# One-core streaming encoder layer: the second block's summed activations formed in the output projection, first column blocks taken out of their banks unscaled, the merge add on VectorE

## The chip, the cores and the metric

The kernel runs on one core of one Trainium2 chip. The metric is the device time of one execution in microseconds. A profile is one separate execution; its rows are times from the start of its span. TensorE (PE) does the matmuls, VectorE (DVE), ScalarE (ACT) and GpSimd (POOL) the elementwise work, SyncE (SP) starts the transfers (DMA). Each engine works through its own list of instructions strictly in order.

## The reference

560 rows (16 meta tokens, 512 prompt rows, 32 sample rows) of 1024 features pass through one layer, all in float32. Cut to what matters here:

```python
def half_step_ffn(x, g, w_gate, w_up, w_down):          # D_MODEL 1024, D_FF 2816
    h = rms_norm(x, g)
    return x + 0.5 * ((silu(h @ w_gate) * (h @ w_up)) @ w_down)
...
x = half_step_ffn(x, ffn1_norm, ffn1_w_gate, ffn1_w_up, ffn1_w_down)      # block 1
... # h @ w_in_all, short convolution, multi-head latent attention
conv_branch = (b_gate * conv_y) @ w_conv_out
mla_branch = attn @ w_mla_out
merged = sigmoid(g_conv) * conv_branch + sigmoid(g_mla) * mla_branch
x = x + merged @ w_out_all                                                # output projection
x = half_step_ffn(x, ffn2_norm, ffn2_w_gate, ffn2_w_up, ffn2_w_down)      # block 2
```

## The kernel before, in words

The residual lies transposed: `y[p, k, t]` holds feature 128k+p of row t, k = 0..7. Block 1 works on all 560 columns in two halves of 280, the output projection and block 2 on 544 columns in two halves of 272.

**Three matmuls for one.** Each float32 operand is split into a rounded part and a rest (`split`, L113: ACT casts the high part, `V.tensor_sub` or GpSimd subtracts for the low part), and `mm3` (L159 to L162) multiplies wh·xh, wh·xl and wl·xh. A weight tile is loaded and split by `load` (L117): DMA `wr`, ACT `wh`, DVE `wl` (128x1024).

**The RMS norm is applied late.** `gained` (L499) leaves gain·y as xh, xl and adds up squares (POOL, `sq`); the factor of each row, 1/rms, comes out of `token_rstd` (L512) and a Newton iteration into `r` (L172 to L178). `spread` (L180) turns `r` into a tile `R` that has the factor on all partitions: matmuls against the identity (L184), then copies out of two banks (L188 to L193). A product of unscaled activations is multiplied by R when it leaves its bank.

**A feed-forward block** is `ffn` (L198). Its 22 blocks of 128 hidden columns make 11 pairs. Pair 0 goes through `plain` (L229): column block j = 0 (gate and up side by side, two accumulators, 96 matmuls), then j = 1 (again 96). In it `before(0)` and `before(1)` are calls of the stage around: in block 1 `before(1)` transposes `craw` and `qkr` (L628, L631), in block 2 it is `spread`; block 1's own spread is at L606, ahead of `before`. Behind each j the banks are emptied by

```python
V.tensor_mul(two(tg), ps[0][:, :, :n], Rv)       # L255: waits for R
S.activation(tg, tg, AF.Silu)
V.tensor_mul(two(tu), ps[1][:, :, :n], two(tg))  # L257
split(ah[:, j], al[:, j], tu)
```

Pairs 1 to 10 go through `job` (L345): one gate job and one up job a pair, seven Winograd products of 12 matmuls instead of eight. Its moving operands are sums of activations, made once a block by `combine` (L264): ACT forms gain·y for k and k+4 into a `tg` tile, DVE makes four sums (L272 to L275), and `split` writes them to xsh, xsl (128x1120 or 128x1088); four combines a block. Its weight sums `ws`, `yl`, `zl` are DVE and ACT work of `operands` (L301). `up_job` (L386) multiplies and splits the result into ah, al, with the subtraction on GpSimd, in three pieces for 544 or 560 columns. `down` (L401) multiplies chunks of pairs with w_down; the last chunk closes each block of y (L430, L431). Behind block 1's last chunk, `done` (L633) also loads `wkv` into the place of xsh and scales it in eight DVE instructions (L651).

**Merge** (L1204). A loop over m = 0..7 makes attn @ w_mla_out (48 matmuls), then

```python
V.tensor_mul(two(sg), ps, two(sg))   # L1243: gate times the branch
GP.tensor_add(sg, sg, cb)            # L1244: plus the convolution branch
split(mh[:, m], ml[:, m], sg)
```

GpSimd also multiplies both gates by R2 and the convolution branch by its gate. The output projection (L1247 to L1252) then takes m = 0..7, k = 0..7 each, and adds `yo`, the residual.

**What sets the order.** The order on each engine is fixed when the program is built, by a scheduler; where the code says "later" it is bound by hand.

Of the kernel before, what the change touches and what calls it, by code (L numbers as in the profile page):

```python
# [1 line left out]

# [10 lines left out]
F32 = mybir.dt.float32  # L13
# [8 lines left out]
P = 128  # L22
# [28 lines left out]
WMAX = KD * P  # L51

# [25 lines left out]
def encoder_step(ctx: ExitStack, tc: tile.TileContext, i, o):  # L78
# [101 lines left out]
    def spread(pa, pb, rstd, R, n=MS, meta_first=False):  # L180
# [12 lines left out]
        V.tensor_copy(R[:, MS:], pa)  # L193
# [4 lines left out]
    def ffn(pool, acc, one, wg, wu, wd, gain, lo, y, R, w0, before, done):  # L198
# [11 lines left out]
        xs = (xh, xl)  # L210
        a = {}
# [7 lines left out]

        def gates():  # L220
            return pool.tile([P, 2, N2], F32, tag="tg", name="tg", bufs=2)
# [7 lines left out]
        def plain(p):  # L229

            ah, al = pair_tiles(p)
            for j in range(2):
                fc = slice(j * P, (j + 1) * P)
                if j == 0:
                    w = w0 or [load([x[:, fc]]) for x in (wg, wu)]
                    ps = [acc(), acc()]
                    order = [(k, q) for k in range(KD) for q in range(2)]
                    if w0:
                        order = [(k, q) for q in range(2) for k in range(KD)]
                    for s, (k, q) in enumerate(order):  # L240
                        for e in range(2):
                            mm3(ps[e][:, q, :n], at_k(w[e], k), at_k(xs, k, cols[q]), k == 0, k == KD - 1)
                        if s == 7:
                            before(0)
                    before(1)
                else:
                    ps = []
                    for x in (wg, wu):
                        w = load([x[:, fc]])
                        ps.append(acc())  # L250
                        for k in range(KD):
                            for q in range(2):
                                mm3(ps[-1][:, q, :n], at_k(w, k), at_k(xs, k, cols[q]), k == 0, k == KD - 1)
                tg, tu = rows(), rows()
                V.tensor_mul(two(tg), ps[0][:, :, :n], Rv)  # L255
                S.activation(tg, tg, AF.Silu)
                V.tensor_mul(two(tu), ps[1][:, :, :n], two(tg))  # L257
                split(ah[:, j], al[:, j], tu)
                yield

        xsh = pool.tile([P, KH, 4, n], F32R, tag="xsh", name="xsh")
        xsl = pool.tile([P, KH, 4, n], F32R, tag="xsl", name="xsl")

        def combine(k):  # L264

            z = gates()
            for j in range(2):
                m = k + j * KH
                S.activation(z[:, j], y[:, m, lo:], AF.Identity, scale=cT[:, gain + m : gain + m + 1])
            c = gates().rearrange("p a (b n) -> p (a b) n", n=n)  # L270
            b11, b12, b21, b22 = (z[:, j // 2, (j % 2) * n : (j % 2 + 1) * n] for j in range(4))
            V.tensor_sub(c[:, 0], b11, b12)  # L272
            V.tensor_sub(c[:, 2], b22, b12)
            V.scalar_tensor_tensor(c[:, 1], c[:, 0], -1.0, b22, op0=ALU.mult, op1=ALU.subtract)
            V.scalar_tensor_tensor(c[:, 3], c[:, 1], -1.0, b21, op0=ALU.mult, op1=ALU.subtract)  # L275
            return split(xsh[:, k], xsl[:, k], c)[1]
# [24 lines left out]
        def operands(raw, after=None):  # L301
# [17 lines left out]
            if after:  # L319
                for x in steps:  # L320
                    tc.add_manual_dep(x.ins, after.ins.name, NOSYNC, reason="later")
# [49 lines left out]

        G = {}

        def gate_job(p, ops):
            def into():
                G[p] = gates()
                return lambda j: G[p][:, j]

            def finish():
                g = G[p]  # L380
                V.tensor_mul(g, g, R[:, None, lo:].to_broadcast([P, 2, N2]))
                S.activation(g, g, AF.Silu)

            return job(p, ops, finish, into)

        def up_job(p, ops):  # L386
# [71 lines left out]
        first = plain(0)  # L458
        next(first)
        for k in range(KH):  # L460
            last = combine(k)
        next(first)
        raws = [fetch(*jobs[0][1:])]
        ops = operands(raws[0], last)
# [3 lines left out]
        for x, (make, w, p) in enumerate(jobs):  # L468
            g = make(p, ops)
# [5 lines left out]
            d = None  # L475
            if make is gate_job and ready:
                d = down(ready, False)
                next(d)
                ready = None
            if x + 1 < len(jobs):  # L480
                ops = operands(raws[x + 1])
# [56 lines left out]
    with ExitStack() as es:  # L538
# [15 lines left out]
        with tc.tile_pool(name="ps0", bufs=4, space=PSUM, reuse_waits="tile") as psum:  # L554
# [43 lines left out]
            for t, step in enumerate((3, 5, 8, 10, 6)):  # L598
                junk = pool.tile([P, D], F32, tag="tg", name="junk", bufs=2)
# [6 lines left out]
            spread(px(), px(), r1, R1, MS, True)  # L606
# [6 lines left out]
        def before(step):  # L613
# [11 lines left out]
            else:  # L625
                n = CC + 16
# [5 lines left out]
                V.tensor_copy(gqk[:QK], ps[:QK, :2])  # L632

        late = {}

        def done(m):
            if m == 0:
                late["yms"] = pool.tile([P, KD, MS], F32, tag="zh", name="yms")
                late["sq"] = pool.tile([P, T], F32, tag="xsl", name="sq")
                late["tmp"] = pool.tile([P, T], F32, tag="tg", name="sqt", bufs=2)  # L640
# [13 lines left out]
        ffn(pool, acc, one, wg, wu, wd, G1, 0, y, R1, w0, before, done)  # L654
# [690 lines left out]
```

## Time and profile before

| | |
|---|---|
| time before, median of 3 runs | 1450.91 us (1448.59 to 1451.77) |
| the profiled execution | 1446.04 us, its span 1444.1 us |
| TensorE | busy 1394.5 us, 97% of the span; granted clock 0.99 in the mean |
| VectorE | 1001.0 us, 69% |
| ScalarE | 652.3 us, 45% |
| GpSimd | 492.8 us, 34% |

Times inside the profile are counted from the start of its span. TensorE's matmuls overlap, so how fast they go is read from how many start in a stretch, not from the duration of one. A granted clock of 1.00 is 2.4 GHz, of 0.50 1.2 GHz.

### The profile page before, as it was taken

The page shows a single profiled execution, that of the slowest core. Times are in us where ns is not written, and L with a number is a line of the kernel's source. Part 1 is how long each engine was busy: PE and PEld are TensorE (multiplying, and loading weights), DVE is VectorE, ACT ScalarE, POOL GpSimd, SP SyncE. Part 2 cuts the span into 40 slices and gives each one's busy share as a digit, 9 for nine tenths or more (in the row PEclk, how much of TensorE's full clock was granted, in tenths as well). Part 3 has the DMA queues.
Part 4 walks back from the last instruction along what each step waited for, and adds up shares of the span by engine and source line. Part 5 has one row for each costly group of instructions (what it writes and reads, how often), then busy time and mean ns, then how long its engine had stood idle before and what let it go on. Part 6 is the DMA issues. An engine that isn't in the chain of part 4 may idle for free.

```text
span 1444.1 us, 26675 instructions
## 1 busy us (share of the span) xinstructions
PE 1394.5 (97%) x10667; PEld 1360.9 (94%) x10667; DVE 1001.0 (69%) x1703; ACT 652.3 (45%) x1220; POOL 492.8 (34%) x731
## 2 busy tenths in 40 slices
PE   7999999999999999999999999998989999999998
PEld 5899999999899999998999999998989999999988
DVE  5887878787566665955955857533587787878744
ACT  6543443434324454453554556533364343434431
POOL 1011111112396864645623424179811021111120
PEclk9999999999999999999999999999999999999999
DMA  6242323233243222222332234355433232324213
GB/s 172 65 125 74 115 66 113 75 102 88 78 131 93 84 79 77 71 60 56 119 90 71 84 120 145 113 175 159 143 95 103 72 107 87 118 68 125 69 44 95
DMA packets 215634, 141.63 MB, mean 98 GB/s; under 512 B 6415, under 2 KB 202914, under 8 KB 215510
## 3 DMA queue, kind: packets, MB, share of 16 engines
q1 hardware_dynamic: 215510, 139.93, 32.8%
q8 instruction: 83, 1.36, 0.4%
q14 instruction: 41, 0.34, 0.1%
HBM read 124.15 MB, written 15.76 MB: 97 GB/s over the span
## 4 chain that ended last, share of the span: by engine, by line
PE 79%; POOL 7%; DVE 6%; issue 4%; DMA 2%; ACT 1%; SPq 0%; POOLq 0%; ACTq 0%; DVEq 0%
PE b L160 9%; PE b L161 9%; PE b L162 9%; PE acc L160 7%; PE acc L161 7%; PE acc L162 7%; PE f L160 6%; PE f L161 6%; PE f L162 6%; POOL sg L71 2%; POOL sq L71 1%; PE t L160 1%; PE t L1168 1%; POOL cb L71 1%; PE late L160 1%
## 5 line engine op out<-in xcount | busy, mean ns | idle before, releaser
L71 POOL TENSOR_TENSOR al<-tu,ah 128x187 fp32r<-128x187 f32 (+3 forms) x120 | 106.5, 919 | 612.7 <-issue 374.5
L114 ACT CAST wh<-wr 128x1024 fp32r<-128x1024 f32 (+2 forms) x165 | 166.6, 1019 | 235.5 <-PE acc L161 128.0
L160 PE MATMUL f<-xh,wh 128*128 128x272 f32 (+1 forms) x816 | 240.2, 295 | 1.5 <-DVE ext L838 1.2
L162 PE MATMUL f<-xh,wl 128*128 128x272 f32 (+1 forms) x816 | 239.1, 293 | 0.0
L161 PE MATMUL f<-xl,wh 128*128 128x272 f32 (+1 forms) x816 | 238.6, 293 | 0.0
L161 PE MATMUL acc<-al,wh 128*128 128x280 f32 (+1 forms) x704 | 203.9, 291 | 2.6 <-POOL al L71 2.6
L160 PE MATMUL acc<-ah,wh 128*128 128x280 f32 (+1 forms) x704 | 203.1, 291 | 2.4 <-DVE tu L430 1.5
L162 PE MATMUL acc<-ah,wl 128*128 128x280 f32 (+1 forms) x704 | 202.9, 291 | 0.3 <-DVE wl L115 0.3
L71 POOL TENSOR_TENSOR wl<-wr,wh 128x256 fp32r<-128x256 f32 x196 | 151.9, 804 | 150.0 <-ACT wh L114 131.1
L115 DVE TENSOR_TENSOR wl<-wr,wh 128x1024 fp32r<-128x1024 f32 (+2 forms) x115 | 141.4, 1236 | 37.4 <-ACT wh L114 32.9
L160 PEld LDWEIGHTS f<-xh,wh 128*128 128x128 f32 x816 | 154.8, 190 | 2.8 <-ACT wh L114 1.4
L161 PEld LDWEIGHTS f<-xl,wh 128*128 128x128 f32 x816 | 154.9, 190 | 0.4
L162 PEld LDWEIGHTS f<-xh,wl 128*128 128x128 f32 x816 | 154.8, 190 | 0.5
L160 PE MATMUL b<-xsh,yh 128*128 128x280 f32 (+1 forms) x480 | 139.1, 290 | 0.7 <-ACT kept L342 0.5
L161 PE MATMUL b<-xsl,yh 128*128 128x280 f32 (+1 forms) x480 | 139.1, 290 | 0.0
L162 PE MATMUL b<-xsh,yl 128*128 128x280 f32 (+1 forms) x480 | 138.9, 289 | 0.1
L161 PEld LDWEIGHTS acc<-al,wh 128*128 128x128 f32 x704 | 132.4, 188 | 3.1 <-POOL al L71 3.0
L160 PEld LDWEIGHTS acc<-ah,wh 128*128 128x128 f32 x704 | 132.0, 188 | 3.4 <-DVE tu L430 1.9
L162 PEld LDWEIGHTS acc<-ah,wl 128*128 128x128 f32 x704 | 132.0, 188 | 0.6 <-DVE wl L115 0.6
L115 DVE TENSOR_TENSOR yl<-ws,yh 128x1024 fp32r<-128x1024 f32 x80 | 103.4, 1293 | 38.0 <-ACT yh L114 37.7
L114 ACT CAST yh<-ws 128x1024 fp32r<-128x1024 f32 x80 | 84.0, 1050 | 92.5 <-PE b L161 84.8
L161 PE MATMUL b<-xl,wh 128*128 128x280 f32 (+1 forms) x320 | 92.5, 289 | 0.0
(358 smaller groups left out, 3826.3 us busy)
## 6 DMA issues: line engine op xcount, KB each, us to landing
wr<-in_w_in_all_dram SPq DMA_DIRECT2D x43, 512.0 KB, 3.9
wr<-in_ffn_w_down_dram SPq DMA_DIRECT2D x32, 512.0 KB, 4.3
wr<-in_ffn_w_gate_dram SPq DMA_DIRECT2D x23, 512.0 KB, 3.9
wr<-in_ffn_w_up_dram SPq DMA_DIRECT2D x23, 512.0 KB, 5.1
wq<-in_ffn_w_gate_dram SPq DMA_DIRECT2D x20, 512.0 KB, 4.2
wq<-in_ffn_w_up_dram SPq DMA_DIRECT2D x20, 512.0 KB, 4.2
wr<-in_ffn_w_down_dram SPq DMA_DIRECT2D x16, 384.0 KB, 3.5
gt_dram<-b SPq DMA_DIRECT2D x16, 272.0 KB, 2.0
```

Of the source, the lines that this page charges most:

```text
L71: last = op(out[:, lo:hi], a[:, lo:hi], b[:, lo:hi])
L114: a = S.copy(hi, src)
L115: return a, (E or V).tensor_sub(lo, src, f(hi))
L160: PE.matmul(out, a[0], b[0], start=start, stop=False, skip_group_check=onto)
L161: PE.matmul(out, a[0], b[1], start=False, stop=False, skip_group_check=onto)
L162: PE.matmul(out, a[1], b[0], start=False, stop=stop, skip_group_check=onto)
L1168: PE.transpose(ps[:, (t - j) * P : (t - j + 1) * P], pw[:, a : a + P], ident)
```

## The change

1. `combine` is pulled out of `ffn` into `summed`. For block 2 the four combines are made in the output projection, which takes its blocks in the order 0, 4, 1, 5, 2, 6, 3, 7: after each second one, features k and k+4 are there. `tg` has three buffers instead of two.
2. The first two projections (m = 0 and 4) are both opened with k = 0..6; k = 7 follows for each.
3. `plain` copies the banks of column block 0 to SBUF unscaled (`S.copy` for gate, `V.tensor_copy` for up) and multiplies by R later; `before(1)`, with the spread of both blocks in it, stands inside column block 1 (behind k = 3 of gate). Block 1's combines come behind the copies of R.
4. Block 1's first gate job (pair 1) is `plain_job`: 96 plain matmuls instead of 84.
5. The merge add is a VectorE instruction. The last up job's `al` is subtracted on VectorE in both blocks.
6. `next(d)`, the load of down's first weights, stands ahead of the gate job.

```diff
+OUT_ORDER = (0, 4, 1, 5, 2, 6, 3, 7)
...
+    def summed(pool, gain, lo, y):
...
+        def combine(k, after=None):
+            z = gates()
...
+            for j in range(2):
+                m = k + j * KH
+                S.activation(z[:, j], y[:, m, lo:], AF.Identity, scale=cT[:, gain + m : gain + m + 1])
+            c = gates().rearrange("p a (b n) -> p (a b) n", n=n)
...
+            made.append(split(xsh[:, k], xsl[:, k], c)[1])
+            if after:
+                for x in made:
+                    tc.add_manual_dep(x.ins, after.ins.name, NOSYNC, reason="later")
...
+            g, u = rows(), rows()
+            S.copy(two(g), ps[0][:, :, :n])
+            V.tensor_copy(two(u), ps[1][:, :, :n])
...
+                    if x is wg and k == 3:
+                        ready = before(1)
+                if x is wg:
+                    V.tensor_mul(g, g, R[:, lo:])
+                    S.activation(g, g, AF.Silu)
+                    V.tensor_mul(u, u, g)
+                    split(ah[:, 0], al[:, 0], u)
+                    ready = [c(ready) for c in combine]
...
+        def plain_job(p, w, finish, into):
+
+            out = into()
+            for j in range(2):
+                ops = load([w[:, (2 * p + j) * P : (2 * p + j + 1) * P]])
+                ps = acc()
+                for k in range(KD):
+                    for q in range(2):
+                        mm3(ps[:, q, :n], at_k(ops, k), at_k(xs, k, cols[q]), k == 0, k == KD - 1)
+                S.copy(two(out(j)), ps[:, :, :n])
+                yield
...
-                    split(ah[:, j], al[:, j], u[j], GP)
+                    split(ah[:, j], al[:, j], u[j], V if p == NF // 2 - 1 else GP)
...
-            spread(px(), px(), r1, R1, MS, True)
...
+                last = spread(one("b1"), one("b2"), r1, R1, MS, True)
...
-            GP.tensor_add(sg, sg, cb)
+            V.tensor_add(sg, sg, cb)
...
-        for m in range(KD):
-            ps = project(i["w_out_all"][0, :, m * P : (m + 1) * P], (mh, ml))
...
+        for j, m in enumerate(OUT_ORDER):
+            if j == 0:
+                opened = [project(w_out(x), (mh, ml), 0, KD - 1) for x in (0, 4)]
+            if j < 2:
+                ps = project(None, (mh, ml), KD - 1, KD, opened[j])
+            else:
+                ps = project(w_out(m), (mh, ml))
...
+            if j % 2:
+                combine[j // 2]()
```

VectorE at the start of block 1, before: `tg`, `xsl` are a combine's tiles, `wl_495` a weight, `acc_278` the gate bank of column block 0, `b_385` and `b_388` the transposes of `before(1)`.

```order
L115 TENSOR_TENSOR wl_495<-wr_493,wh_494 128x1024
L193 COPY R1_84<-px_261 128x512
L115 TENSOR_TENSOR xsl_275<-tg_401,xsh_274 128x1120
L188 COPY R1_84<-px_262 128x48
L272 TENSOR_TENSOR tg_411<-tg_408 128x280
L273 TENSOR_TENSOR tg_411<-tg_408 128x280
L255 TENSOR_TENSOR tu_391<-acc_278,R1_84 128x560
L629 COPY cT_70<-b_385 128x59
L632 COPY gqk_78<-b_388 96x2
```

The same place in the changed kernel, from the last step of the Newton iteration (L180); `acc_270` is the up bank of column block 0.

```order
L180 SCALAR_TENSOR_TENSOR r1_75<-nrb_250,r1_75 128x5
L550 MEMSET ms_4680 128x5
L278 COPY tu_377<-acc_270 128x560
L664 COPY cT_70<-b_420 128x59
L667 COPY gqk_78<-b_423 96x2
L117 TENSOR_TENSOR wl_497<-wr_495,wh_496 128x1024
L195 COPY R1_84<-b1_411 128x512
L218 TENSOR_TENSOR tg_458<-tg_455 128x280
```

The bank is emptied ahead of the copies of R, the transposes' copies too, and no combine stands ahead of any of them.

VectorE at the end of block 1, before: `tu_4037`, `tu_4038` are the last up job's two results, `acc_4145` the first bank of the last `down` chunk.

```order
L396 TENSOR_TENSOR tu_4037<-tu_4037,tg_3905 128x560
L368 TENSOR_TENSOR tu_4038<-b2_4036,kept_4110 128x280
L396 TENSOR_TENSOR tu_4038<-tu_4038,tg_3905 128x560
L651 TENSOR_SCALAR wkv_4257<-wkv_4257,cT_70 128x160 x8
L430 SCALAR_TENSOR_TENSOR tu_4251<-acc_4145,R1_84 128x560
L430 SCALAR_TENSOR_TENSOR tu_4278<-acc_4214,R1_84 128x560
```

The same place in the changed kernel.

```order
L433 TENSOR_TENSOR tu_4028<-tu_4028,tg_3896 128x560
L391 TENSOR_TENSOR tu_4029<-b2_4027,kept_4101 128x280
L433 TENSOR_TENSOR tu_4029<-tu_4029,tg_3896 128x560
L117 TENSOR_TENSOR al_4188<-tu_4028,ah_4187 128x560
L687 TENSOR_SCALAR wkv_4244<-wkv_4244,cT_70 128x160 x8
L117 TENSOR_TENSOR al_4188<-tu_4029,ah_4187 128x560
L467 SCALAR_TENSOR_TENSOR tu_4238<-acc_4136,R1_84 128x560
```

Both subtractions for `al` are now on VectorE, one ahead of the eight instructions on `wkv`, one behind them.

VectorE in the changed kernel from the second to last output block (`late_12340` is its bank) on: combine 3 of block 2 (`tg_12469`) lies between the residual adds and the weights of block 2.

```order
L1303 TENSOR_TENSOR y_11285<-late_12340,yo_12389 128x544
L117 TENSOR_TENSOR wl_12494<-wr_12492,wh_12493 128x1024
L538 SCALAR_TENSOR_TENSOR xl_74<-y_11285,cT_70,xh_73 128x544
L218 TENSOR_TENSOR tg_12469<-tg_12466 128x272
L1303 TENSOR_TENSOR y_11285<-late_12406,yo_12455 128x544
L117 TENSOR_TENSOR wl_12624<-wr_12622,wh_12623 128x1024
L538 SCALAR_TENSOR_TENSOR xl_74<-y_11285,cT_70,xh_73 128x544
L219 TENSOR_TENSOR tg_12469<-tg_12466 128x272
```

And further on, where column block 0 of block 2 is emptied (`acc_12499` is its up bank, `r3` the row factors):

```order
L117 TENSOR_TENSOR yl_12772<-ws_12758,yh_12771 128x1024
L178 TENSOR_TENSOR nra_12594<-r3_77 128x5
L278 COPY tu_12619<-acc_12499 128x544
L179 SCALAR_TENSOR_TENSOR nrb_12595<-nra_12594,ms_12585 128x5
L117 TENSOR_TENSOR wl_12693<-wr_12691,wh_12692 128x1024
L180 SCALAR_TENSOR_TENSOR r3_77<-nrb_12595,r3_77 128x5
L117 TENSOR_TENSOR wl_12760<-wr_12753,wh_12759 128x1024
L178 TENSOR_TENSOR nra_12594<-r3_77 128x5
```

Before, the combines and the copies of R stood between this bank's last matmul and its emptying; now one weight's low part (`yl_12772`) stands ahead of the copy.

## Rows read from the trace of the kernel before

**Rows 1.** The page, part 1: span, and each engine's busy time, share and instructions.

```profile
span 1444.1 us, 26675 instructions
...
PE 1394.5 (97%) x10667; PEld 1360.9 (94%) x10667; DVE 1001.0 (69%) x1703; ACT 652.3 (45%) x1220; POOL 492.8 (34%) x731
```

**Rows 2.** Windows: us; busy of PE, PEld, DVE, ACT, POOL; granted clock; DMA; GB/s.

```profile
...
37.03:43.86 6.83, 5.79 (x26) 5.79 (x26) 6.11 (x13) 3.66 (x5) 0.00 (x0) 0.50 0.12 35
100.00:120.00 20.00, 20.00 (x157) 20.00 (x157) 14.47 (x18) 5.38 (x6) 0.00 (x0) 1.00 0.30 86
960.00:980.00 20.00, 20.00 (x162) 20.00 (x161) 8.35 (x8) 7.43 (x10) 20.00 (x30) 1.00 0.63 192
999.59:1006.42 6.83, 4.99 (x22) 4.99 (x23) 2.54 (x3) 1.95 (x3) 6.83 (x11) 0.50 0.55 161
1067.86:1071.27 3.41, 3.41 (x17) 3.41 (x16) 2.77 (x5) 2.60 (x3) 0.00 (x0) 0.50 0.00 0
```

**Rows 3.** Waits of TensorE, 30 to 40 us: total us, times, longest.

```profile
...
PE b L628 <- DVE R L188: 2.1, 1, 2.1
PE acc L160 <- DVE tu L255: 1.0, 1, 1.0
```

**Rows 4.** Timeline of TensorE, 31 to 39 us: start, us, instruction, [idle before].

```profile
...
33.10 1.48 PE L184 MATMUL px<-ident,r 128*128 128x128 f32 x10 [0.46 <-DVE ms L515]
...
38.08 0.60 PE L160 MATMUL acc<-xh,wh 128*128 128x280 f32 x1 [1.03 <-DVE tu L255]
```

**Rows 5.** Waits of TensorE, 380 to 388 us.

```profile
...
PE acc L161 <- POOL al L71: 1.3, 1, 1.3
PE acc L160 <- DVE tu L430: 0.8, 1, 0.8
```

**Rows 6.** Waits of TensorE, 990 to 1003 us.

```profile
...
PE late L160 <- ACT mh L114: 5.4, 1, 5.4
```

**Rows 7.** Waits of TensorE, 1048 to 1095 us.

```profile
...
PE acc L160 <- DVE tu L255: 2.7, 1, 2.7
...
PE b L184 <- DVE r L178: 1.0, 1, 1.0
```

**Rows 8.** Timeline of TensorE, 1399 to 1405 us.

```profile
...
1403.02 0.40 PE L161 MATMUL acc<-al,wh 128*128 128x272 f32 x1 [1.26 <-POOL al L71]
```

**Rows 9.** Timeline of VectorE, 30 to 40 us.

```profile
...
35.14 1.31 DVE L115 TENSOR_TENSOR xsl<-tg,xsh 128x1120 fp32r<-128x1120 f32 x1
```

**Rows 10.** Timeline of VectorE, 380 to 392 us.

```profile
...
383.59 2.82 DVE L651 TENSOR_SCALAR wkv<-wkv,cT 128x160 f32<-128x160 f32 x8 [1.49 <-DMA wkv<-in_w_in_all_dram]
386.33 1.38 DVE L430 SCALAR_TENSOR_TENSOR tu<-acc,R 128x560 f32<-128x560 f32 x2
```

**Rows 11.** Timeline of VectorE, 1060 to 1082 us.

```profile
...
1066.82 0.43 DVE L272 TENSOR_TENSOR tg<-tg 128x272 f32<-128x272 f32 x1
...
1069.31 0.73 DVE L115 TENSOR_TENSOR al<-tu,ah 128x544 fp32r<-128x544 f32 x1 [0.36 <-ACT ah L114]
1070.31 1.29 DVE L115 TENSOR_TENSOR xsl<-tg,xsh 128x1088 fp32r<-128x1088 f32 x1 [0.28 <-ACT xsh L114]
```

**Rows 12.** Timeline of ScalarE, 994 to 1013 us.

```profile
...
1009.70 0.65 ACT L114 CAST mh<-sg 128x544 fp32r<-128x544 f32 x1 [2.57 <-POOL sg L71]
```

**Rows 13.** Groups of VectorE by form, 1010 to 1050 us.

```profile
...
L115 DVE TENSOR_TENSOR wl<-wr,wh 128x1024 fp32r<-128x1024 f32 x8 | 11.6, 1457 | 3.3 <-ACT wh L114 3.3
L503 DVE SCALAR_TENSOR_TENSOR xl<-y,cT,xh 128x544 fp32r<-128x544 f32 x7 | 7.1, 1019 | 0.0
L1251 DVE TENSOR_TENSOR y<-late,yo 128x544 f32<-128x544 f32 x8 | 5.7, 720 | 12.6 <-PE late L162 12.6
```

**Rows 14.** Groups of VectorE by form, 955 to 995 us: busy us, mean ns, idle before.

```profile
...
L115 DVE TENSOR_TENSOR wl<-wr,wh 128x1024 fp32r<-128x1024 f32 x6 | 9.3, 1552 | 6.2 <-ACT wh L114 6.2
L115 DVE TENSOR_TENSOR ml<-sg,mh 128x544 fp32r<-128x544 f32 x5 | 5.0, 1001 | 8.2 <-ACT mh L114 8.2
```

**Rows 15.** Groups of VectorE by form, 100 to 200 us.

```profile
...
L115 DVE TENSOR_TENSOR wl<-wr,wh 128x1024 fp32r<-128x1024 f32 x12 | 14.6, 1221 | 1.2 <-ACT wh L114 1.2
```

More of the change, by code (lines that the diff above doesn't have):

```diff
@@ L210, in ffn @@
         xs = (xh, xl)
+        gates, (xsh, xsl), combine = sums
         a = {}
@@ L231, in plain @@
             ah, al = pair_tiles(p)
[L232 to L276, printed above, removed]
+            w = w0 or [load([x[:, :P]]) for x in (wg, wu)]
@@ new lines, in plain @@
+            ps = [acc(), acc()]
+            order = [(k, q) for k in OUT_ORDER for q in range(2)]
+            if w0:
+                order = [(k, q) for q in range(2) for k in range(KD)]
+            for s, (k, q) in enumerate(order):
+                for e in range(2):
+                    mm3(ps[e][:, q, :n], at_k(w[e], k), at_k(xs, k, cols[q]), k == 0, k == KD - 1)
+                if s == (7 if w0 else 13):
+                    before(0)
+            g, u = rows(), rows()
+            S.copy(two(g), ps[0][:, :, :n])
@@ L278, in moving @@
+            g, u = rows(), rows()
+            V.tensor_mul(two(g), ps[0][:, :, :n], Rv)
+            S.activation(g, g, AF.Silu)
+            V.tensor_mul(two(u), ps[1][:, :, :n], two(g))
+            split(ah[:, 1], al[:, 1], u)
+            return ready
         def moving(what):
@@ L457, in ffn @@
         jobs = [(make, w, p) for p in range(1, NF // 2) for make, w in ((gate_job, wg), (up_job, wu))]
[L458 to L464, printed above, removed]
+        made = plain(0)
+        ops, raws = None, [None]
+        if not made:
+            raws = [fetch(*jobs[0][1:])]
+            ops = operands(raws[0])
         raws.append(fetch(*jobs[1][1:]))
@@ L468, in ffn @@
         for x, (make, w, p) in enumerate(jobs):
+            d = None
+            if make is gate_job and ready:
+                d = down(ready, False)
+                next(d)
+                ready = None
             g = make(p, ops)
@@ L474, in ffn @@
             pending = g
[L475 to L479, printed above, removed]
             if x + 1 < len(jobs):
-                ops = operands(raws[x + 1])
+                ops = operands(raws[x + 1], made and x == 0 and made[-2:])
             if x + 2 < len(jobs):
@@ L652, in done @@
                 GP.memset(kvt[:, 4], 0.0)
[L654 removed]
+        ffn(pool, acc, one, wg, wu, wd, 0, y, R1, w0, summed(pool, G1, 0, y), before, done)
         sq, wkv, yms = late["sq"], late["wkv"], late["yms"]
@@ L1292, in encoder_step @@
             pool, acc, one, i["ffn2_w_gate"][0], i["ffn2_w_up"][0], i["ffn2_w_down"][0],
-            G2, META, y, R3, None, before, done,
+            META, y, R3, None, sums, before, done,
         )
```

69 lines of the change are left out of this document (52 added, 17 removed).

## The prediction

> **What bounds the kernel now.** I read the page's busy times first, then the waits of TensorE stage by stage, then the clock in windows. TensorE is busy for 1394.5 of 1444.1 us [rows 1]; the other engines have room, so time can only come from TensorE's idle stretches, from its clock, or from the number of its matmuls. With nothing in the way 157 matmuls of 280 columns start in 20 us, 0.127 us each, and 162 of 272 columns, 0.1235 us each [rows 2]. The idle time lies in a few places. Column block 1 of block 1 starts only at 38.08 us, behind waits of 0.46, 2.1 and 1.03 us [rows 3, 4]. The end of block 1 has waits of 1.3 and 0.8 [rows 5], the output projection one of 5.4 [rows 6], the start of block 2 waits of 1.0 and 2.7 [rows 7], the end of block 2 one of 1.3 [rows 8]. Three of these stretches are followed by one at a granted clock of 0.50, the 1.2 GHz level: 6.83 us from 37.03, 6.83 from 999.59, 3.41 from 1067.86 [rows 2]. TensorE was busy there for 5.79, 4.99 and 3.41 us; 26 matmuls in 5.79 us are 0.223 each. At full clock the same work would take about 0.127/0.223 = 0.57 of that, so these stretches cost 2.5, 2.1 and 1.5 us beside the waits.
>
> **Start of block 1.** Before, the bank of column block 0 is freed by a product with R (L255), and VectorE has a weight, the copies of R and a combine ahead of it (one `xsl` is 1.31 us, [rows 9]). In the changed kernel the order shows the copy of the bank and the two small copies directly behind the Newton iteration, the combines behind R. I expect the transposes of `craw` right behind column block 0, and the spread (1.48 us, [rows 4]) already when the first bank is being copied, since it only waits for `r`. Its 1.48 us are paid as before. So of 0.46 + 2.1 + 1.03 = 3.6 us about 0.3 stay: minus 3.3. If TensorE does not idle there, I expect the clock to stay at 1.00: minus 2.5. The plain gate job has 12 matmuls more: plus 12 x 0.127 = 1.5. The unscaled copies cost the path nothing: ScalarE's and VectorE's run side by side under the spread and the transposes; uncovered, one 560-element pass would be about 0.7, half of the 1.38 for two passes of that size [rows 10]. Block 1's combines now have a column block and a plain job of cover, two times 12.2 us of TensorE; if they were late, each would show as one `xsl` of 1.31. Together **minus 4.3**, bounds minus 8 (the small waits for weights near here go as well; not counted) and minus 1 (the clock falls all the same and one `xsl` is in the way).
>
> **End of block 1.** This is the place where the change costs. The second `al` stands behind the eight `wkv` instructions, and these wait for a DMA: VectorE sat idle for 1.49 us and then scaled from 383.59 until 386.41 [rows 10]. Only then comes the second `al`, some 0.73 us (the same subtraction on 544 elements, [rows 11]), so 387.1. Behind it in the queue are the emptyings of both opened banks (L430). Before, GpSimd made this `al` meanwhile, and TensorE's last wait here, for the first emptying, ended at 386.33 + 0.7 = 387.0. Now the matmuls that need `al` start only at 387.1, about a dozen until both banks are complete, 1.5 us, and the third bank's start moves from 387.0 to about 388.6: plus 1.6. A longer single wait also risks a 3.41 us stretch at half clock, 1.5 us [rows 2], which I take at one half. **Plus 2.3**, bounds 0 (if the transfer lands earlier) and plus 4.5.
>
> **Merge and output projection.** The 5.4 us wait is for `mh`, behind GpSimd's last adds: the last `mh` cast starts at 1009.70 [rows 6, 12], while GpSimd has not an idle moment from 960 to 980 and is busy throughout the slow stretch [rows 2]. The eight merge adds are a quarter of its 32 operations here (per m two gates times R2, the convolution branch times its gate, the add, each in three pieces). Without them GpSimd is done about a quarter earlier; and TensorE asks for feature 7 only behind 84 matmuls of the two opened projections, 10.4 us later than it starts. Both make the wait go: minus 5.4, and minus 2.1 if the clock stays up. On VectorE an add of this size is 0.72 [rows 13], in a stage in which it is busy for 8.35 of 20 us [rows 2]: covered by the matmuls; uncovered at the last m, 0.72 once, and that lies under the opened projections.
>
> Here row and page pull against the change. VectorE's 128x1024 subtraction takes 1.552 us while GpSimd works without pause and 1.221 where it mostly rests [rows 14, 15]; the 544-element one took 1.001 there, against 0.73 [rows 11]. The Trainium skill, "GPSIMD Engine Reference", section Specifications, says that GpSimd shares its SBUF interfaces with VectorE and that they contend where a VectorE instruction has two SBUF inputs; the rows agree. By it the moved add, which has two, would slow both engines. Taken from the rows the eight adds cost 8 x 0.28 = 2.2 us more of VectorE's time, in a stage where it is idle for more than half: nothing on the path here; where VectorE is fuller, in the output projection, the slowing makes the second rival below.
>
> **Start of block 2.** The combines are done by then. Minus 1.0 (the spread now stands inside column block 1, after `r` is ready) and minus 2.7 (no `tu` behind R), minus 1.5 for the clock. What comes new: the copy of the up bank (L278) stands behind `yl` (one of 1024 elements, 1.2 [rows 15]) and takes 0.7, so gate of column block 1, which needs the banks, waits about 1.2. The spread's 1.5 us stay. **Merge to here: minus 5.4 - 2.1 - 1.0 - 2.7 - 1.5 + 1.2 = minus 11.5**, bounds minus 13 and minus 6 (clock not recovered, copy 2 us late).
>
> **End of block 2.** No `wkv` there, two `al` of 0.73 in a row instead of GpSimd's pieces: **minus 0.9** of the 1.3 [rows 8], bounds minus 1.3 and 0.
>
> The earlier `next(d)` only moves loads forward under matmuls: nothing, or half a us each way.
>
> Sum: -4.3 + 2.3 - 11.5 - 0.9 = -14.4, with a little for the small waits, **minus 15**. The profiled 1446.04 would become 1431; the median before is 1450.91, 4.9 above the profiled execution, and becomes **1436 us**. All bounds at once would be 1450.9 - 22.3 = 1429 and 1450.9 - 2.5 = 1448.
>
> **Rivals.**
> *The waits go, the clock does not come back* (or falls in new places): the sum loses 2.5 + 2.1 + 1.5 = 6.1, so 1442. For it: the stretches lie behind other, smaller waits too, such as the new 1.2 at block 2. Against: two of the three waits that lie ahead of them go wholly.
> *VectorE becomes the bound of the output projection.* A pair of projections is 96 x 0.1235 = 11.9 us on TensorE. VectorE has then two residual adds (1.44), two `xl` (2.04), two weights (2.91) [rows 13], four sums (1.7) and one `xsl` (1.29) [rows 11]: 9.4. With the strongest slowing that the rows show, 1.001/0.73 = 1.37, it is 12.9, 1.0 over in each of four pairs, and it reaches the start of block 2 late by a `tg` group (3.0): plus 7, so 1443.
> *Slower than before*, by the same mechanism: VectorE would have to need 15/4 = 3.8 more than 11.9 in each pair, 15.7, a factor of 1.67 on 9.4; with a factor of 1.75 the pairs cost 4 x 4.5 = 18, so 1454. Against it: no row of a long group here shows more than 1.37, and GpSimd has lost work.
>
> **How the numbers follow.** I give the forecast 0.68 (its own range 1430 to 1440), the clock rival 0.16, VectorE as bound 0.10, slower 0.03, and 0.03 that the gains and the losses cancel. Low is 1429, where all terms go to their good bounds; high 1444, above both middle rivals. A difference within 0.2%, 2.9 us, is about what a measurement of this kernel can't tell from none: faster 0.92, same 0.04, slower 0.04.
>
> **What would show it.** Right: column block 1 of block 1 starting near 34.4 instead of 38.08 and granted clock 1.00 behind it; the second `al` behind `wkv` at about 387 in times of before, and TensorE waiting more than 2 us there for VectorE; no wait for `mh` in the output projection, and its 384 matmuls in about 47.5 us; a wait of about a us for `tu` at L278, and the first Winograd job of block 2 some 11 to 12 us nearer to the start of the merge's last matmul. Wrong: a stretch at 0.50 in a new place; waits of TensorE for VectorE's residual adds or `wl` in the output projection; combines that reach into block 2.

## The result, and the profile after

The median is 1433.62 us (1432.14 to 1435.51, 4 runs) beside 1450.56 us for the kernel before (1448.59 to 1451.77): ratio 0.9885, 95% interval 0.9868 to 0.9902. In a later series on one chip the same kernel (`control`, below) had 1436.14 against 1448.40, ratio 0.991 (0.9895 to 0.9925). The forecast was 1436, range 1429 to 1444.

The page of the changed kernel, part 1, to be read beside [rows 1]:

```profile
span 1431.6 us, 26658 instructions
...
PE 1388.9 (97%) x10679; PEld 1356.4 (95%) x10679; DVE 1010.9 (71%) x1708; ACT 650.7 (45%) x1218; POOL 477.4 (33%) x695
```

TensorE has 12 matmuls more and is still busy for 5.6 us less, since less of its work is done at half clock. Where the rest went is seen if the span is cut at matmuls that both traces have (starts, in us, of the first `down` matmul, the first of `wkv`, of w_mla_out, of the output projection, of block 2, of block 2's Winograd products, of the output's transposes):

| stage | before | after | difference | predicted |
|---|---|---|---|---|
| up to the first `down` matmul of block 1 | 77.14 | 70.36 | -6.8 | -4.3 |
| rest of block 1 | 337.97 | 339.10 | +1.1 | +2.3 |
| attention | 527.00 | 526.03 | -1.0 | 0 |
| w_mla_out | 49.48 | 49.54 | +0.1 | 0 |
| output projection | 56.26 | 53.63 | -2.6 | -7.5 |
| start of block 2 | 32.87 | 30.13 | -2.7 | -4.0 |
| rest of block 2 | 330.73 | 330.10 | -0.6 | -0.9 |

The sum of the differences is -12.5, as the spans say (1444.1 and 1431.6), against the prediction's -14.4: a sum that is nearly right, by stages that were wrong in opposite directions. The first row is the best case. The other nine profiles whose four engines have the same order up to 370 us (the control and eight of the experiments) put the first `down` matmul at 70.64 to 72.34: a gain of 4.8 to 6.5, against one profile of the kernel before.

Start of block 1, timeline of TensorE (start, us, instruction). The transposes and the spread follow the last matmul of column block 0, and column block 1 starts at 34.13 with no wait at all, where it waited three times before [rows 3, 4]:

```profile
...
32.41 0.22 PE L663 MATMUL b<-ident,craw 67*128 67x67 f32 x1
...
32.69 1.51 PE L186 MATMUL b<-ident,r 128*128 128x128 f32 x10
34.13 0.40 PE L162 MATMUL acc<-xh,wh 128*128 128x280 f32 x1
```

Windows of the changed kernel (columns as in [rows 2]): the stretch that ran at 0.50 is at 1.00, 55 matmuls instead of 26. The second row, in the output projection, still is at 0.50, for half as long as before:

```profile
...
37.03:43.86 6.83, 6.83 (x55) 6.83 (x54) 6.51 (x12) 5.84 (x8) 0.00 (x0) 1.00 0.39 110
993.11:996.53 3.42, 3.07 (x13) 3.07 (x14) 3.06 (x5) 1.03 (x2) 1.26 (x2) 0.50 0.51 153
```

End of block 1: waits of TensorE from 374 to 425 us, then VectorE's timeline there, beside [rows 5, 10]. The second `al` does stand behind `wkv`, and TensorE waits for it, 1.4 of the 2.4 us. But the eight `wkv` instructions take 1.79 us, not 2.82:

```profile
...
PE acc L163 <- DVE al L117: 2.4, 2, 1.4
...
PE acc L552 <- POOL sq L73: 0.5, 3, 0.2
...
PE acc L162 <- DVE tu L467: 0.2, 1, 0.2
...
377.21 1.79 DVE L687 TENSOR_SCALAR wkv<-wkv,cT 128x160 f32<-128x160 f32 x8 [0.82 <-DMA wkv<-in_w_in_all_dram]
378.92 0.74 DVE L117 TENSOR_TENSOR al<-tu,ah 128x560 fp32r<-128x560 f32 x1
```

Output projection, waits of TensorE, beside [rows 6]. The wait for `mh` is halved, not gone; it is for feature 6 now, asked for behind 36 matmuls:

```profile
...
PE late L162 <- ACT mh L116: 2.9, 1, 2.9
PE late L163 <- DVE ml L117: 0.5, 1, 0.5
```

Before, it was for feature 5, and not for the last cast at 1009.70 [rows 12]: TensorE's wait ended at 1001.43, with this cast, the sixth of eight (ScalarE, kernel before):

```profile
...
1000.74 0.65 ACT L114 CAST mh<-sg 128x544 fp32r<-128x544 f32 x1 [2.02 <-POOL sg L71]
```

Start of block 2, beside [rows 7], and end of block 2, beside [rows 8]:

```profile
...
PE acc L162 <- DVE tu L278: 2.4, 1, 2.4
PE acc L162 <- DVE y L1303: 0.5, 1, 0.5
...
PE acc L163 <- DVE al L117: 0.9, 1, 0.9
```

The wait for the emptied bank is 2.4 us where 1.2 was expected. The one for `al` is 0.9 where 1.3 less 0.9 was expected; the wait behind it, for the first emptying, fell too, from 0.66 to 0.19.

### The profile page after: what moved, and what is told of

Read it like the earlier page. It is cut to its first block, busy times and chain, and to the rows that moved or that the text cites. A ratio compares the mean times of both kernels' runs of the same rounds, so it can differ in the third digit from the quotient of the medians.

```text
span 1431.6 us, 26658 instructions
## 1 busy us (share of the span) xinstructions
PE 1388.9 (97%) x10679; PEld 1356.4 (95%) x10679; DVE 1010.9 (71%) x1708; ACT 650.7 (45%) x1218; POOL 477.4 (33%) x695
## 4 chain that ended last, share of the span: by engine, by line
PE 82%; POOL 6%; DVE 5%; DMA 3%; issue 2%; ACT 1%; SPq 0%; POOLq 0%; ACTq 0%; DVEq 0%
PE b L162 10%; PE b L163 9%; PE b L164 9%; PE acc L162 8%; PE acc L163 8%; PE acc L164 7%; PE f L162 6%; PE f L163 6%; PE f L164 6%; POOL sg L73 2%; POOL sq L73 1%; PE t L162 1%; PE late L163 1%; PE t L1204 1%; PE late L162 1%
## 5 line engine op out<-in xcount | busy, mean ns | idle before, releaser
L73 POOL TENSOR_TENSOR al<-tu,ah 128x187 fp32r<-128x187 f32 (+3 forms) x108 | 98.5, 945 | 568.5 <-issue 340.6
L163 PE MATMUL b<-xsl,yh 128*128 128x272 f32 (+1 forms) x468 | 135.6, 290 | 0.0
L162 PE MATMUL b<-xsh,yh 128*128 128x272 f32 (+1 forms) x468 | 135.6, 290 | 0.0
L164 PE MATMUL b<-xsh,yl 128*128 128x272 f32 (+1 forms) x468 | 135.4, 289 | 0.0
L467 DVE SCALAR_TENSOR_TENSOR tu<-acc,R 128x560 f32<-128x560 f32 (+1 forms) x80 | 58.2, 730 | 46.5 <-PE acc L164 46.3
```

What stands on the lines that cost most here:

```text
L73: last = op(out[:, lo:hi], a[:, lo:hi], b[:, lo:hi])
L162: PE.matmul(out, a[0], b[0], start=start, stop=False, skip_group_check=onto)
L163: PE.matmul(out, a[0], b[1], start=False, stop=False, skip_group_check=onto)
L164: PE.matmul(out, a[1], b[0], start=False, stop=stop, skip_group_check=onto)
L467: V.scalar_tensor_tensor(t, ps[:, :, :n], 0.5, Rv, op0=ALU.mult, op1=ALU.mult)
```

## Why `mh` is still late: GpSimd beside VectorE

GpSimd's part of the merge, timeline (groups of pieces), and VectorE's, of the same stretch:

```profile
...
940.56 1.65 POOL L73 TENSOR_TENSOR sg<-sg,R 128x181 f32<-128x181 f32 x3 [33.02 <-DMA sg<-gt_dram]
...
953.72 6.81 POOL L73 TENSOR_TENSOR sg<-sg,R 128x181 f32<-128x181 f32 x9
...
991.28 3.09 POOL L73 TENSOR_TENSOR cb<-cb,sg 128x181 f32<-128x181 f32 x3
...
952.87 0.72 DVE L1282 TENSOR_TENSOR sg<-late,sg 128x544 f32<-128x544 f32 x1 [1.16 <-ACT sg L1270]
953.79 1.08 DVE L1283 TENSOR_TENSOR sg<-sg,cb 128x544 f32<-128x544 f32 x1 [0.20 <-POOL cb L73]
954.79 1.60 DVE L117 TENSOR_TENSOR wl<-wr,wh 128x1024 fp32r<-128x1024 f32 x1
956.32 1.09 DVE L117 TENSOR_TENSOR ml<-sg,mh 128x544 fp32r<-128x544 f32 x1
```

Read one by one in the trace, a piece takes 0.57 us when nothing disturbs it: three are 1.65 us. The group of nine from 953.72 on takes 6.81 us, because three VectorE instructions with two SBUF inputs lie in it: the merge add (544 elements), a `wl` (1024), an `ml` (544). The piece that meets one of 544 takes 1.06 us, the one that meets a `wl` 1.56; the product out of the bank (L1282) at 952.87 lengthens none. The add itself takes 1.08 instead of 0.72. Seven of the eight moved adds lengthen a piece so, by 0.49 us each, 3.4 together (the eighth, at 994.41, comes behind the last piece), against the 24 pieces that the move saves, 13.2 at 1.65 for three. GpSimd also stands idle for 1.5 us at 942.2, for a gate's transfer. Its chain from first to last piece is 53.8 us long (940.56 to 994.37); before it was 62.6 (947.11 to 1009.67).

The Trainium skill's rule that the prediction named ("GPSIMD Engine Reference", section Specifications) covers just this, and the trace agrees: 0.57 us becomes 1.06 or 1.56. The prediction priced VectorE's side of it only.

## The experiments

Theory after the result: the merge is still paced by GpSimd, which VectorE's two-input instructions hold up; what gained are the unscaled copies and the shorter chain on GpSimd. The main rival: what gained are the early sums and the opened projections.

**add_pool**: the merge add back on GpSimd.

```diff
-            V.tensor_add(sg, sg, cb)
+            GP.tensor_add(sg, sg, cb)
```

> The changed kernel with the eight merge adds back on GpSimd; all else as changed (the scheduler is free to order anew, and puts TensorE's first projections in pieces again). Theory: GpSimd's chain in the merge is what the wait for mh ends on, and the adds cost it 24 pieces. Then the chain from its first piece to its last is near 62 us as before (53.8 in the changed kernel), TensorE idles 5 us or more in the output projection instead of 3.35, and half clock follows for 6.83 us instead of 3.41: 1436 to 1441 us. Rival, that opening two projections alone shortened the wait: 1433 to 1434, idle time there as in the changed kernel.

Measured: 1442.72 us, ratio to before 0.9961 (0.9941 to 0.998). TensorE waits 6.82 us in one piece, until the cast from 1000.43 on; GpSimd had been idle for 5.83 us on the way there:

```profile
...
1000.43 0.64 ACT L116 CAST mh<-sg 128x544 fp32r<-128x544 f32 x1 [2.02 <-POOL sg L73]
...
1001.13 0.59 PE L162 MATMUL late<-mh,wh 128*128 128x272 f32 x1 [6.82 <-ACT mh L116]
...
966.64 5.03 POOL L73 TENSOR_TENSOR sg<-sg,R 128x181 f32<-128x181 f32 x9 [5.83 <-DMA sg<-gt_dram]
```

The output projection takes 60.3 us, against 53.6 in the changed kernel and 56.3 before, with 10.2 us at half clock. It is slower than expected, and not by the add alone: in the order that the scheduler made anew, SyncE issues the gate's transfer at 962.40, behind a weight's that waits for VectorE until 961.91. Neither the kernel before nor the changed one has this idle stretch. Without it the wait would be about 1 us (an estimate, 6.82 less 5.83). So this run doesn't show what the moved add gained by itself.

**not_opened**: projections one after the other.

```diff
-            if j < 2:
-                ps = project(None, (mh, ml), KD - 1, KD, opened[j])
-            else:
-                ps = project(w_out(m), (mh, ml))
+            ps = project(w_out(m), (mh, ml))
```

> The changed kernel, with the first two output projections written one after the other (k = 0..7 each). Theory: the wait for feature 6 stays as it is (2.9 us, since both orders ask for it behind 36 matmuls), and TensorE waits once more, for feature 7, about 1.6 us: 1435 us. Rival, that the two opened projections carry most of the gain in the merge: 5 us or more of idle time in place of 3.35, 1437 or more. A third possibility, that opening does nothing because another engine ends last anyway: 1433.6.

Measured: 1437.95 us, ratio 0.9923 (0.9906 to 0.9941). TensorE's timeline, the rows with a wait:

```profile
...
993.90 0.39 PE L162 MATMUL late<-mh,wh 128*128 128x272 f32 x1 [2.70 <-ACT mh L116]
...
997.16 0.82 PE L162 MATMUL late<-mh,wh 128*128 128x272 f32 x2 [0.90 <-ACT mh L116]
```

The wait for feature 6 is as it was, and one of 0.9 us for feature 7 is added, with 6.8 us at half clock instead of 3.4. The idle time is as the theory had it, the total as the rival had it (1437 or more). The output projection takes 55.7 us: 2.1 above the changed kernel's, most of it by the clock, and only 0.5 below that before. In these single profiles the opened projections carry more of the stage's 2.6 us than the moved add without them. In the kernel before they were half there already: its scheduler had interleaved the first two projections by itself.

**k6_k7_late**: feature 6 asked for later.

```diff
-                opened = [project(w_out(x), (mh, ml), 0, KD - 1) for x in (0, 4)]
+                opened = [project(w_out(x), (mh, ml), 0, KD - 2) for x in (0, 4)]
+                opened = [project(None, (mh, ml), KD - 2, KD - 1, x) for x in opened]
```

> The changed kernel, but the two opened projections run k = 0..5 first, then k = 6 of both, then k = 7 of both, so that feature 6 is asked for behind 72 matmuls instead of 36. Theory: feature 6 was asked for 3 us before it was there, feature 7 is the later only by 3 us: the wait of 2.87 and the 0.48 behind it shrink to 0.8 or less, and no half clock follows: 1429 to 1431 us. Rival, that the chain through GpSimd moves with TensorE (its gates wait for what TensorE frees), so that the wait only moves to feature 7: 1433.

Measured: 1434.52 us, ratio 0.9905 (0.9883 to 0.9926). The waits for `mh` and `ml` are gone; two others stand in their place, for the second projection's weight:

```profile
...
995.46 0.39 PE L162 MATMUL late<-mh,wh 128*128 128x272 f32 x1 [0.85 <-ACT wh L116]
...
997.01 0.40 PE L164 MATMUL late<-mh,wl 128*128 128x272 f32 x1 [1.03 <-DVE wl L117]
```

1.9 us instead of 3.3, and half clock behind them again; the output projection takes 52.3 us. Neither theory had this wait: SyncE issues that weight's transfer behind those of the gates, at 991.00, and ScalarE casts it at 994.38, right behind a sigmoid that waited for GpSimd. Beside its neighbours the total can't be told from the changed kernel's.

**add_psum**: the gated product stays in its bank, so that the add has one SBUF input.

```diff
-            V.tensor_mul(two(sg), ps, two(sg))
-            V.tensor_add(sg, sg, cb)
+            V.tensor_mul(ps, ps, two(sg))
+            V.tensor_add(two(sg), ps, two(cb))
```

> The changed kernel, with the gated product left in its bank (VectorE multiplies in place in PSUM) and the merge add reading the bank and cb, so one SBUF input instead of two. Theory: a VectorE instruction with two SBUF inputs lengthens the GpSimd piece beside it by its own length (0.57 to 1.06 us under an add of 544 elements, to 1.56 under 1024; a product out of a bank does not). Then the eight adds no longer do so: GpSimd's 72 pieces end 3 to 4 us earlier, their mean falls from 0.75 to about 0.70, the add itself takes 0.72 to 0.8 instead of 0.99, the wait for feature 6 falls from 2.87 to under 0.7: 1429 to 1431 us. Rival, that GpSimd is slowed by transfers or by its own turn-around: mean 0.75 as before, 1433 to 1434; an instruction that reads and writes a bank may also be slower, then 1434.

Measured: 1431.12 us, ratio 0.9877 (0.9849 to 0.9906). One group of GpSimd and the add, first in the changed kernel, then here (busy us, mean ns, idle before):

```profile
...
L73 POOL TENSOR_TENSOR sg<-sg,R 128x181 f32<-128x181 f32 x32 | 23.1, 744 | 34.5 <-DMA sg<-gt_dram 34.5
...
L1283 DVE TENSOR_TENSOR sg<-sg,cb 128x544 f32<-128x544 f32 x8 | 7.9, 993 | 6.5 <-POOL cb L73 6.5
```

```profile
...
L73 POOL TENSOR_TENSOR sg<-sg,R 128x181 f32<-128x181 f32 x32 | 19.2, 622 | 34.5 <-DMA sg<-gt_dram 34.4
...
L1283 DVE TENSOR_TENSOR sg<-late,cb 128x544 f32<-128x544 f32 x8 | 5.8, 724 | 6.7 <-POOL cb L73 6.5
```

and all that TensorE waits for in the output projection:

```profile
...
PE late L163 <- DVE ml L117: 0.8, 1, 0.8
```

The add is back at 0.72, the pieces of this group fall from 744 to 622 ns in the mean (all 72 pieces from 766 to 719, 3.4 us together: what the seven adds had cost), the wait for `mh` is gone and no half clock follows: the output projection takes 49.4 us instead of 53.6, and 49.2 in the two runs below that have this edit too, where the control has 53.5. The total alone can't show it, since the intervals overlap. This run shows the first half of the theory, that VectorE's two-input adds hold GpSimd and with it the merge up, since nothing changed but where the product lies. It doesn't weigh the moved add against the opened projections.

**control**, **three_edits**: the changed kernel again; and three edits on it, `add_psum`'s and these two:

```diff
-                    V.tensor_scalar_mul(wkv[:, k], wkv[:, k], cT[:, GM + k : GM + k + 1])
+                    x = V.tensor_scalar_mul(wkv[:, k], wkv[:, k], cT[:, GM + k : GM + k + 1])
+                    tc.add_manual_dep(x.ins, closed[1].ins.name, NOSYNC, reason="later")
...
+            if last:
+                tc.add_manual_dep(steps[-1].ins, last.ins.name, NOSYNC, reason="later")
```

(`closed[1]` is the emptying of the second opened bank in `down`, `last` the copy of the up bank, `steps[-1]` the third Winograd weight's low part.)

> The changed kernel itself again, as the measure for the runs beside it on the same chip: 1431 to 1435 us. Its idle times as in its first profile (2.9 and 0.5 us in the output projection, 2.4 for the copy of the up bank, 1.0 and 1.4 for al at the end of block 1); the number of half-clock stretches may differ.

> The changed kernel with three edits: the gated product stays in its bank and the merge add reads it there; the eight wkv instructions come behind the emptyings of the two opened banks; the copy of block 2's up bank comes ahead of the low part of the third Winograd weight. Theory: the wait for the second al at the end of block 1 falls from 1.4 to 0.3 or less (1.2 gained), the output projection takes 49.4 instead of 53.6 us (4.2), the wait for the copy falls from 2.4 to 0.9 (1.5): 6 to 7 us less than the changed kernel on the same chip, 1425 to 1428. Rival, that what is taken from these waits comes back as others behind them (wl of the last down chunk behind wkv, the third Winograd weight at block 2's first job): 2 us or less.

Measured: control 1436.14 us (ratio 0.991, 0.9895 to 0.9925), three edits 1431.35 (0.9883, 0.987 to 0.9897): 4.8 us, not 6 to 7. Waits of TensorE at the end of block 1, and VectorE's timeline at the start of block 2, with three edits:

```profile
...
PE acc L556 <- POOL sq L73: 1.6, 3, 1.3
PE acc L163 <- DVE al L117: 1.0, 1, 1.0
...
1052.45 0.17 DVE L174 TENSOR_SCALAR r<-ms 128x5 int32<-128x5 int32 x1
...
1053.45 0.17 DVE L179 SCALAR_TENSOR_TENSOR nrb<-nra,ms 128x5 f32<-128x5 f32 x1
1053.54 0.72 DVE L280 COPY tu<-acc 128x544 f32<-128x544 f32 x1
```

The second `al` is in time, but a wait for GpSimd's sums of squares (1.3 us) appears at 419 us, and 6.8 us at half clock follow instead of 3.4: this edit's gain was given back, as the rival had it. The copy (L280) got ahead of the weight, but behind the Newton steps, which wait for one another: it ended 0.5 us earlier at most.

**al_pool**: the last `al` on GpSimd again.

```diff
-                    split(ah[:, j], al[:, j], u[j], V if p == NF // 2 - 1 else GP)
+                    split(ah[:, j], al[:, j], u[j], GP)
```

> The changed kernel with the last al of both blocks back on GpSimd. Theory: at the end of block 1 the place costs little either way, since without GpSimd at work the wkv instructions take 1.79 us and not 2.82: with al on GpSimd they take 2.6 to 2.8 again, TensorE waits 1.3 + 0.8 us there instead of 1.0 + 1.4 + 0.2, so the start of the third bank comes 0.4 to 0.9 us earlier; at the end of block 2 it waits 1.3 + 0.7 instead of 0.9 + 0.2, 0.9 us more. The prediction's own term would have the end of block 1 2.3 us faster. Total: within 1 us of the changed kernel.

Measured, one run: 1440.76 us. VectorE's `wkv` and TensorE's waits at the end of block 1:

```profile
...
378.04 2.82 DVE L687 TENSOR_SCALAR wkv<-wkv,cT 128x160 f32<-128x160 f32 x8 [1.28 <-DMA wkv<-in_w_in_all_dram]
...
PE acc L163 <- POOL al L73: 1.3, 1, 1.3
PE acc L162 <- DVE tu L467: 0.7, 1, 0.7
```

With GpSimd at work beside them the `wkv` instructions take 2.82 us again. From the end of the last Winograd product to the third bank TensorE needs 6.2 us, in the changed kernel 7.0: the place costs 0.8 us, not 2.3. At the end of block 2 it waits 1.26 + 0.67 us instead of 0.93 + 0.19. The total is 4.6 us above the control's median, where at most 1 was expected, the span 2.7 us above that of the control's profile. Block 2's rest is 3.3 us longer (0.8 of it these waits, the rest mostly a half-clock stretch behind them), the output projection 1.9, which the scheduler ordered a little differently; block 1 is 3.2 us shorter, the attention 0.6 longer. One run doesn't tell more.

**win_gate**: block 1's first gate job as Winograd products.

```diff
-        ops, raws = None, [None]
-        if not made:
-            raws = [fetch(*jobs[0][1:])]
-            ops = operands(raws[0])
+        raws = [fetch(*jobs[0][1:])]
+        ops = operands(raws[0], made and made[-2:])
```

> The changed kernel with block 1's first gate job as Winograd products again (84 matmuls instead of 96), its sums made where the changed kernel makes them. Theory: the job starts near 46.6 us and wants the first sums 3 us later, while VectorE has the last of the four ready only near 58: TensorE waits 4 to 8 us there, against 1.5 us for 12 matmuls saved, so 2 to 6 us slower, perhaps with a half-clock stretch. Rival, that the sums are there in time: 1.5 us faster, and the plain job was pure cost.

Measured, one run: 1443.56 us, 7.4 above control. TensorE's waits where the job starts, and what ScalarE did ahead of them:

```profile
...
51.11 0.40 PE L162 MATMUL b<-xh,wh 128*128 128x280 f32 x1 [2.54 <-ACT wh L116]
...
53.93 0.60 PE L164 MATMUL b<-xh,wl 128*128 128x280 f32 x1 [1.34 <-DVE wl L117]
...
47.89 1.11 ACT L116 CAST xsh<-tg 128x1120 fp32r<-128x1120 f32 x1
...
50.01 1.99 ACT L116 CAST wh<-wr 128x1024 fp32r<-128x1024 f32 x2
```

The waits are at the low end of the expected 4 to 8 us (2.5 + 0.2 + 1.3, then 6.8 us at half clock), the total is above the expected 2 to 6, and the place was another: the job waits for its weights, whose casts stand on ScalarE behind the casts of the sums. By this one run the plain job's 12 matmuls are a price well paid, in this order; with the weights' casts put first it was not tried.

**sums_late**: block 2's sums made as block 1's.

```diff
-        sums = gates, X, []
+        sums = gates, X, combine
...
-            if j % 2:
-                combine[j // 2]()
```

> The changed kernel with block 2's four sums taken out of the output projection and made as block 1's are: behind the copies of R, under column block 1, and the first gate job of block 2 as plain_job (96 matmuls instead of 84). Theory: what the sums in the output projection save is these 12 matmuls, 1.5 us, and little else, since the unscaled copies already keep VectorE's sums away from the bank: the output projection stays at 53 to 54 us, the first up job of block 2 starts 13 to 14 us later than the first gate job does now: 1.5 us slower than the changed kernel's 1433.6 to 1436.1. Rival A, that forming them early carries the gain of this stage: waits of 3 us or more and a half-clock stretch at the start of block 2, 5 us slower. Rival B, that the sums hold GpSimd's squares and VectorE's residual adds up in the output projection: same or faster than the changed kernel.

Measured: 1436.18 us, ratio 0.992 (0.9904 to 0.9936). TensorE's waits at the start of block 2:

```profile
...
PE acc L162 <- DVE tu L295: 1.1, 1, 1.1
PE acc L162 <- DVE tu L278: 0.8, 1, 0.8
```

A third as long for the bank as in the changed kernel, with 1.1 us behind column block 1 instead. From the output projection to the output's transposes it takes 417.1 us, the changed kernel 413.9 (the control's profile 414.8); 12 matmuls are 1.5 of the difference. So the part after which the change is named is worth 2.4 to 3.2 us by the profiles; by the total it can't be told from the control.

**scaled_banks**: column block 0 emptied by products with R.

```diff
-            S.copy(two(g), ps[0][:, :, :n])
-            V.tensor_copy(two(u), ps[1][:, :, :n])
+            V.tensor_mul(two(g), ps[0][:, :, :n], Rv)
+            S.activation(g, g, AF.Silu)
+            V.tensor_mul(two(u), ps[1][:, :, :n], two(g))
```

> The changed kernel, but column block 0 of both blocks is emptied as before the change, by products with R (the spread again ahead of them), while the sums stay where the change puts them. Theory: the unscaled copies are what removes the waits at the start of both blocks. Then column block 1 waits for R again: about 2.7 us in block 1 (weight, copies of R, three sums' steps and the product ahead on VectorE), 3 to 4 us in block 2 (Newton steps, spread, copies), with half clock behind each: 8 to 10 us slower than the changed kernel, 1442 to 1446. Rival, that moving the sums out of the way was the gain and the copies add little: 2 us slower or less.

Measured: 1437.84 us, ratio 0.9935 (0.9918 to 0.9951). In block 1 the wait is back, 2.96 us with 3.4 us at half clock behind it:

```profile
...
37.40 0.57 PE L162 MATMUL acc<-xh,wh 128*128 128x280 f32 x1 [2.96 <-DVE tu L278]
```

The first `down` matmul starts at 74.23, 1.9 to 3.9 us after those of the ten profiles above. In block 2 the expectation was too high: the scheduler put the first Winograd products where TensorE would have waited, and the block loses 1.6 us beside the first profile, 0.6 beside the control's. So the total is well under the expected 1442 to 1446.

**psum_copy**: `add_psum`, and the copy of block 2's up bank ahead of the Newton steps too.

```diff
+            for x in [] if w0 else newton:
+                tc.add_manual_dep(x.ins, copied.ins.name, NOSYNC, reason="later")
```

> The changed kernel with two edits: the merge add reads the gated product from its bank, and in block 2 the copy of the up bank comes ahead of the Newton steps and of the third Winograd weight; the wkv instructions stay as in the changed kernel (moved, they gave their gain back at the sums of squares). Theory: the wait for the copy falls from 2.2 (2.0 with the copy only ahead of the weight, behind the Newton steps of 0.17 us that each wait for the one before) to about 1.0, the output projection stays at 49.4 us: 5 to 6 us under the changed kernel, 1429 to 1431, and no slower than the kernel with three edits (1431.35). Rival, that the row factors then come late to the spread inside column block 1: a wait of 1 us or more there, and 1432 to 1434.

Measured: 1429.38 us (1425.18 to 1430.74), ratio 0.9866 (0.9846 to 0.9885), the lowest of all. The wait for the copy, at the start of block 2:

```profile
...
PE acc L162 <- DVE tu L281: 0.8, 1, 0.8
```

0.8 instead of 2.4 us, and no wait at the spread. Its interval lies well below 1; it overlaps the changed kernel's own of the first series, and lies below that of the control.

## Why the prediction was right, point by point

**Start of block 1: right, mis-sized.** -6.8 instead of -4.3 in the first profile, -4.8 to -6.8 in ten. The waits went to zero, not to 0.3, and most of the small waits behind (1.2 us in the trace of before, 0.5 after), which the prediction left out, went too. `scaled_banks` shows that without the unscaled copies 1.9 to 3.9 us of it are lost, `win_gate`, in one run, that the plain job is needed for it.

**End of block 1: right in the mechanism, mis-sized.** +0.7 at the place itself (7.0 instead of 6.3 us), not +2.3. The price of the eight `wkv` instructions, which have one tensor input each, was taken from a row in which GpSimd's `al` pieces ran beside them; the change itself removes these. No half clock followed in the first profile; in that of the control it did.

**Merge: the step that failed** is "Without them GpSimd is done about a quarter earlier; and TensorE asks for feature 7 only behind 84 matmuls [...] Both make the wait go". GpSimd's chain became 8.8 us or a seventh shorter, since the adds hold it up from VectorE's side (3.4 us) and a transfer came late (1.5), and feature 6, not 7, is the one that is asked for too early. The step began with a misreading: before, too, the wait was not for the last cast but for feature 5's, at 1000.74. The prediction's "nothing on the path here" for the slowing was wrong for the same reason. `add_psum` gives back what was missing. How much of the 2.6 us is the moved add's alone stays open. The second rival (VectorE as the bound of the output projection) didn't come: TensorE waits for no weight there, and for a residual add only 0.5 us, behind the last projection.

**Start of block 2.** The waits around the spread are gone, as predicted. The copy's wait was 2.4, twice the forecast: the third weight's `yl` had itself waited for its cast and started only at 1053.22, after the bank's last matmul. Here the order showed what stands ahead, but not when that starts.

**End of block 2: right in size**, -0.8 at the place, but 0.3 of it at the wait for `al` and 0.5 at the emptying behind, which the prediction left out.

**The sum** came out within 2.4 us in part by luck. In the profiles the start of block 1 gave 2.5 more and the end of block 1 cost 1.2 less than thought, the attention gave 1.0 that was not predicted, while merge and block 2's start gave 6 less: -12.5 in all, not -14.4. The medians differ by 16.9 us in the first series and by 12.3 in the later one. The first rival (the clock does not come back) was true of one of its three stretches in the first profile: after 993.11 it fell again, for half as long.

## What to carry to other kernels

When work moves from GpSimd to VectorE, price both sides: in these traces a VectorE instruction with two SBUF inputs holds up the GpSimd piece beside it (0.57 us becomes 1.06 or 1.56), one whose second input lies in PSUM doesn't, so that leaving a product in its bank until the next operation was worth 4.2 us of the stage. A price taken from a trace holds only as long as what ran beside it is still there after the change. And of an opened accumulation, look at every feature that is late, not only at the last one.

## What was not expected of the hardware

Executions of one kernel differ in the number of half-clock stretches. The profile of the control has four that the first profile of the same kernel lacks (windows, columns as in [rows 2]):

```profile
...
28.58:31.99 3.41, 3.30 (x14) 3.29 (x15) 2.70 (x12) 2.47 (x7) 0.00 (x0) 0.50 0.25 75
383.56:386.97 3.41, 3.41 (x16) 3.41 (x16) 3.41 (x6) 1.83 (x3) 1.36 (x2) 0.50 0.15 44
660.04:666.87 6.83, 6.06 (x24) 4.83 (x25) 4.06 (x8) 2.41 (x4) 2.67 (x4) 0.50 0.54 152
1059.40:1062.81 3.41, 3.41 (x17) 3.41 (x16) 2.45 (x9) 0.00 (x0) 0.00 (x0) 0.50 0.53 154
```

In all, ahead of the output, 23.9 us at 0.50 against 10.2, and a span of 1436.3 against 1431.6 us. One of them (660.04) comes with a wait of 2.7 us that all thirteen profiles have, in the attention; four of them fall to 0.50 there, the kernel before among them. In the first profile of the changed kernel the clock stays at 1.00 behind the same wait, which is enough for the 1.0 us that the table above shows for attention. So a kernel's gain in half-clock time is seen in the median of many runs, not by two profiles. What decides whether a stretch follows a given wait was not tried.
